# Steps for the compression rows and the query blocks in the mixing stage of a hybrid decoder block

## The chip, the cores and the metric

The kernel runs on one core of one Trainium2 chip. The metric is the device time of one execution in microseconds, as the median of several runs.

## The reference

The reference is one decoder layer on 512 positions of width 1024, in float32. It adds half a SwiGLU, then a mixing stage, then another half SwiGLU, then a gated embedding:

```python
h = h + 0.5 * swiglu(rmsnorm(h, norm_ffn1), ...)
z = rmsnorm(h, norm_mix) @ w_in        # q | k, v of three branches | gates | u
o = concat(nsa_attention(...), s5_mixer(u, ...))
h = h + o @ w_out
h = h + 0.5 * swiglu(rmsnorm(h, norm_ffn2), ...)
h = h + sigmoid(rmsnorm(h) @ w_ple_gate) * (p @ w_ple)
```

The attention has 8 heads of 64 in 2 groups, and three branches: compressed keys and values, selected blocks, and a window. At 512 positions with 8 blocks of 64 the selection takes all of them. The compressed branch takes windows of 32 positions, 16 apart (31 windows), adds a position table to each, and passes each window of 32 × 64 numbers through a small network with a gelu:

```python
blk = kv[:, tok] + pe                 # tok: 31 windows of 32 positions
compressed = gelu(blk @ w1) @ w2
```

The S5 mixer is a linear recurrence over time in 32 groups, then a gelu, and its output is gated: `y * sigmoid(y @ w_glu + b_glu)`.

## The kernel before

All products run on PE by one helper (`mm`, L133). Where full precision is needed, a float32 matrix is split in a part `hi`, that PE's fast form takes exactly, and a rest `lo`: ACT makes `hi` (L164), DVE makes `lo` (L166), and a product is three products. Raw weights (tile `raw`) come on ACT's DMA queue (L107). Most other transfers of the mixing stage go on SP's queue, in the order of its instructions.

The stages follow each other: the first SwiGLU to about 355 us, the mixing stage to about 604, the first half of the out product and the embedding to about 640, the second SwiGLU to about 995, the gate and the last norm to the end. The change lies in the mixing stage. That stage is a set of Python generators, each of which issues some instructions between two `yield`s:

- `s5_input` and `s5_all` (u, s): the S5 input and recurrence, in eight chunks (`s5_in`, L972 to L992, with the DVE operations L982 to L988 of tiles `t` and `vv`; `s5_out`, L998 to L1010; `s5_back`, L1016 to L1021, which makes the four tiles `yt`).
- `rotary` (L1044) and `keys` (k, L1059): projections, turned, sent to `qd` and `kd` in HBM, and for keys loaded back in four blocks `kf` of two transfers each. ACT makes `KA` (L1066), DVE `KB` (L1067).
- `cmp_kv` (z, L1072): the compression's keys and values, stored to `kcd` (L1082) and `vcd` (L1087).
- `v_gates` (v, L1091): values and gates, four blocks of 24 products each. DVE's L1106 and L1108 empty the sum's bank.
- `cmp_all` (c, L1130): the compression. `windows` (L1114) loads a source twice for each of the two groups, the second time shifted by a position, into tile `cst` (tags r1 and r2), and adds the position table on DVE (L1125) into tiles `cs` (keys) and `turn` (values). Then follow 32 products with `raw` in eight steps, a gelu, a transposition, the tile `chid` (npool's tag "acc", one buffer), and the products of `w2` and `chid` that make `KAc`, its copy `KBc` and `VLc`.
- `glu` (g, L1175): the gelu of the four `yt` tiles, in four steps with scratch `gt` (L916 to L924: Square on ACT, L922 on DVE, Tanh on ACT, L924 on DVE), then four sums of four products `yt`, `raw` in float32. The scratch takes the tags r1 and r2 in turn, the same as `cst`.
- `out_half` (f, L1195): the out product on the S5 half, eight blocks of 12 products.
- `queries` (p, L1219), once for each of the four blocks of 128 queries: loads the 4 heads of each half from `qd` twice, into partitions 0 to 63 and 64 to 127 of a tile `qf` (tag "ra", two buffers, shared with `kf`, the tiles of L1076 and L1086 and others). ACT scales into `QA` and `QB`, DVE makes the rest into the upper half of `QA` (L1240).
- `scores` (t, L1244): for each block and head the scores, a maximum on DVE (L1261) and exponentials on ACT (L916), of which only the sums are kept. `compressed` (x, L1267) does the same with `KAc`.
- `values` (V, L1326): the second pass with the sums known. PE makes scores into `ps_C` or `ps_B`, ACT exponentials `e` and `eh`, DVE `el` (L1359), PE the products with `VL` or `VLc` into `ps_D`.

The order in which the generators' steps are written is the table `PLAN` (L1590): each word is one step of one generator, with the block's number behind p, t, x, V. This order fixes which tile takes which buffer. A list scheduler then puts each engine's instructions into the order in which they will stand in the program, so that neither order is the same as `PLAN`.

Of the kernel before, what the change touches and what calls it, by code (L numbers as in the profile page):

```python
# [19 lines left out]
SEQ = 512  # L20
# [56 lines left out]
def block_kernel(ctx: ExitStack, tc: tile.TileContext, a: dict, out: bass.AP):  # L77
    nc = tc.nc
    V, S, G, PE = nc.vector, nc.scalar, nc.gpsimd, nc.tensor
# [15 lines left out]
    h = pers.tile([128, KT, SEQ], F32, name="h")  # L95
# [751 lines left out]
    def mixer(ctx):  # L847
# [7 lines left out]
        ind = mp.tile([128, 128], FR, name="ind")  # L855
# [61 lines left out]

        def gelu2(o, x, w, tag):

            t = tp.tile([128, SEQ], F32, tag=tag, name="gt")[:, :w]  # L920
            act(t, x, AF.Square)
            V.scalar_tensor_tensor(t, t, 1 / 0.044715, x, OP.add, OP.mult)  # L922
            act(t, t, AF.Tanh, scale=math.sqrt(2 / math.pi) * 0.044715)
            V.scalar_tensor_tensor(o, t, 1.0, x, OP.add, OP.mult)  # L924
# [189 lines left out]
        def windows(src, i, dst):  # L1114
            ev = []
            for g in range(2):
                st = tp.tile([128, SEQ], F32, tag=f"r{g + 1}", name="cst")
                nc.sync.dma_start(st[0:64], src[g])
                nc.sync.dma_start(st[64:128, 0:SEQ - 1], src[g, :, 1:SEQ])
                ev.append(st.rearrange("p (j l r) -> p l j r", l=8, r=2)[:, :, :, 0])  # L1120
            sp = []
            for half, t in enumerate(dst):
                t = t.rearrange("p (l g j) -> p l g j", l=8, g=2)
                for g in range(2):
                    V.tensor_tensor(t[:, :, g], ev[g],  # L1125
                                    pe[:, i, 8 * half:8 * half + 8, None].to_broadcast([128, 8, 32]), OP.add)
                sp.append(t)
            return sp

        def cmp_all():  # L1130

            kt = [tp.tile([128, SEQ], F32, tag=n, name="cs") for n in ("rb1", "r3")]
            sps = windows(kcd.rearrange("(g r) a t -> g (r a) t", g=2), 0, kt), windows(vcd, 1, (cosr, sinr))
            yield
            ps = bank("A", (128, 256))
            for l in range(16):
# [23 lines left out]
            kah = KAc[:, 0:128].rearrange("p (g i j) -> p g i j", g=2, i=2)  # L1160
            S.copy(kah[0:64, :, 0, 0:31], p)
            S.copy(kah[64:128, :, 0, 0:31], p)
            V.tensor_tensor(kah[0:64, :, 1, 0:31], p, kah[0:64, :, 0, 0:31].bitcast(F32), OP.subtract)
            for g in range(2):
                V.tensor_copy(KBc[0:64, :, g, 0:31],
                              kah[0:64, g:g + 1, 1, 0:31].bitcast(F32).to_broadcast([64, 4, 31]))
            for g in range(2):
                p = bank("D", (31, 64))
                for m in range(2):
# [46 lines left out]
        nmax = mp.tile([128, 4, 3, 8], F32, name="nmax")  # L1216
        den = mp.tile([128, 4, 3, 8], F32, name="den")

        def queries(qb, pool):  # L1219

            tq = slice(qb * 128, (qb + 1) * 128)
            QA = pool.tile([128, 8, 128], FR, tag="QA", name="QA", bufs=2)
            QB = pool.tile([128, 8, 128], FR, tag="QB", name="QB", bufs=2)
            envs[qb].update(QA=QA, QB=QB)
            if qb > 1:
                S.copy(QB[64:128], ind[64:128, None, :].bitcast(F32).to_broadcast([64, 8, 128]))
            else:

                G.dma_start(QB[64:128], ind[64:128, None, :].to_broadcast([64, 8, 128]))
            for i, (hs, st) in enumerate(zip((slice(0, 4), slice(4, 8)), STAGE[qb])):  # L1230
                src = qd[i].rearrange("(h r) a t -> (r a) h t", h=4)[:, :, tq]
                if st == "ra":
                    qf = mp.tile([128, 4, 128], F32, tag=st, name="qf", bufs=2)
                else:
                    qf = tp.tile([128, 4, 128], F32, tag=st, name="qf")
                nc.sync.dma_start(qf[0:64], src)
                nc.sync.dma_start(qf[64:128], src)
                S.activation(QA[:, hs], qf, AF.Copy, scale=0.125)
                S.activation(QB[0:64, hs], qf[0:64], AF.Copy, scale=0.125)
                V.scalar_tensor_tensor(QA[64:128, hs], qf[64:128], 0.125, QA[64:128, hs].bitcast(F32),  # L1240
                                       OP.mult, OP.subtract)
                yield

# [82 lines left out]
        def values(qb, env):  # L1326
# [3 lines left out]
            for g in range(2):  # L1330
# [39 lines left out]
                for par in range(2):  # L1370
# [7 lines left out]
        envs = {qb: {} for qb in range(4)}  # L1378
        gens = dict(u=s5_input(), k=keys(), q=rotary("q0", qd[0], TQ[0]), Q=rotary("q1", qd[1], TQ[1]), z=cmp_kv(),
                    v=v_gates(), s=s5_all(), c=cmp_all(), g=glu(), f=out_half(range(4, 8)))  # L1380
        made = {"p": lambda b: queries(b, mp if b > 1 else ap_), "t": lambda b: scores(b, TS[b]),
                "x": lambda b: compressed(b), "V": lambda b: values(b, envs[b])}
        table.append(tc.keep_in_program_order(S.preload_act_table_set("exp_and_others")))
        for step in PLAN.split():
# [195 lines left out]
TU, TQ, TW, TY, TP = "AD", "AA", "C", "D", "D"  # L1580

TS = "AB", "AB", "BC", "BBBBBBBBBCBCBCBC"
GT = "r1", "r2"
STAGE = ("ra", "ra"), ("ra", "ra"), ("ra", "ra"), ("ra", "ra")

PLAN = """u u u k s s u k k q s q s Q p3 s s s k s Q s t3 t3 s t3 z t3 s s t3 s p3 s z t3 t3 s s t3 t3 s g t3 g t3 g t3
v t3 c v v c t3 v c c p2 t2 t3 t3 t2 p2 c c c t2 c c t2 t2 c v t2 t2 t2 t2 t2 t2 t2 t2 t2 g close p1 p1 p0 x3  # L1590
# [169 lines left out]
```

## Time and profile before

| | us |
|---|---|
| median of 3 runs | 1046.03 |
| runs | 1049.57, 1046.03, 1044.05 |
| the profiled execution | 1045.87 |
| its span in the profile | 1044.1 |
| PE busy | 1030.6 |
| DVE busy | 823.1 |
| ACT busy | 502.0 |
| POOL busy | 160.5 |

The profile is of one execution. Its rows give a start, a duration, the engine (PE, PEld for the weight load that runs beside PE, DVE, ACT, POOL, SP; SPq is the time in which SP issues a DMA), the line of the kernel and the tiles, out<-in. A bracket holds the idle time ahead of it and what ended it. PE's durations overlap, since products are pipelined.

The mean granted clock of PE is 0.997 of full speed.

### The profile page before, as it was taken

The numbers are of one execution on the slowest core, as the hardware profiler recorded it, in microseconds if no ns is written. First come the engines' busy times: TensorE is split into PE (matmuls) and PEld (weight loads), VectorE is DVE, ScalarE is ACT, GpSimd is POOL, SyncE is SP. The second block draws the span as 40 slices with busy tenths as digits, with TensorE's granted clock in tenths as the row PEclk, the third lists the DMA queues.
The fourth block names the chain that finished last, engine by engine and source line by source line (L and its number), as shares of the span: only waits on it lengthen the run. The fifth ranks groups of instructions, "written<-read, shape, count | busy, mean of one in ns | idle before, by whom it ended". The sixth has DMA issues, their size and how long they took to land.

```text
span 1044.1 us, 15711 instructions
## 1 busy us (share of the span) xinstructions
PE 1030.6 (99%) x6049; PEld 876.9 (84%) x6049; DVE 823.1 (79%) x1381; ACT 502.0 (48%) x868; POOL 160.5 (15%) x181
## 2 busy tenths in 40 slices
PE   9999999999999999999999999999999999999997
PEld 7888888889889888776586688898899899899886
DVE  6798468988989766896689887996598588587666
ACT  6322232535336542477768855653365246245452
POOL 0003948207870200100000000000000000000001
PEclk9999999999999999999999999999999999999999
DMA  7424325636354648766610023434234333333412
GB/s 265 144 91 128 99 89 171 226 121 129 119 138 146 227 122 226 209 194 171 200 41 21 20 61 121 132 111 121 85 100 121 101 102 101 101 102 101 133 69 81
DMA packets 53114, 131.55 MB, mean 126 GB/s; under 512 B 10800, under 2 KB 19664, under 8 KB 53040
## 3 DMA queue, kind: packets, MB, share of 16 engines
q10 hardware_dynamic: 26352, 90.77, 27.4%
q0 software_dynamic: 6592, 18.48, 7.0%
q1 hardware_dynamic: 20096, 21.31, 6.7%
q8 instruction: 47, 0.77, 0.3%
q14 instruction: 27, 0.22, 0.1%
HBM read 114.39 MB, written 15.73 MB: 125 GB/s over the span
## 4 chain that ended last, share of the span: by engine, by line
PE 85%; DVE 5%; POOL 3%; DMA 3%; ACT 2%; issue 2%; SPq 0%; DVEq 0%; ACTq 0%; POOLq 0%
PE ps_A L133 25%; PE ps_C L133 24%; PE ps_B L133 20%; PE ps_D L133 15%; POOL ft L721 1%; POOL bt L720 1%; DMA qf<-qd 1%; DMA qd<-r 1%; DVE lo L166 1%; DMA kf<-kd 1%; DVE el L1359 0%; DMA cst<-kcd 0%; POOL ft L719 0%; DVE s L342 0%; POOL seen L559 0%
## 5 line engine op out<-in xcount | busy, mean ns | idle before, releaser
L164 ACT CAST hi<-raw 128x1024 fp32r<-128x1024 f32 (+2 forms) x143 | 144.4, 1010 | 253.3 <-PE ps_C L133 92.5
L133 PE MATMUL ps_C<-hq,hi 128*128 128x512 f32 x704 | 217.5, 390 | 0.2
L166 DVE TENSOR_TENSOR lo<-raw,hi 128x1024 fp32r<-128x1024 f32 (+2 forms) x143 | 173.4, 1213 | 42.5 <-ACT hi L164 41.5
L133 PEld LDWEIGHTS ps_C<-hq,hi 128*128 128x128 f32 x704 | 130.8, 188 | 28.1 <-DVE h L526 1.4
L133 PE MATMUL ps_C<-hq,lo 128*128 128x512 f32 x352 | 136.9, 389 | 0.0
L133 PE MATMUL ps_A<-xh,hi 128*128 128x512 f32 (+1 forms) x352 | 124.8, 355 | 0.4 <-ACT hi L164 0.4
L133 PE MATMUL ps_A<-xl,hi 128*128 128x512 f32 (+1 forms) x352 | 123.9, 352 | 0.0
L133 PE MATMUL ps_A<-xh,lo 128*128 128x512 f32 (+1 forms) x352 | 122.9, 352 | 0.2 <-DVE lo L166 0.2
L164 ACT CAST hi<-s 128x1024 fp32r<-128x1024 f32 x56 | 58.9, 1053 | 107.0 <-PE ps_D L133 60.9
L166 DVE TENSOR_TENSOR lo<-s,hi 128x1024 fp32r<-128x1024 f32 x56 | 70.6, 1261 | 20.3 <-ACT hi L164 20.2
L133 PEld LDWEIGHTS ps_C<-hq,lo 128*128 128x128 f32 x352 | 66.1, 188 | 13.8
L133 PEld LDWEIGHTS ps_A<-xh,hi 128*128 128x128 f32 x352 | 66.6, 189 | 10.3 <-ACT hi L164 0.7
L133 PEld LDWEIGHTS ps_A<-xh,lo 128*128 128x128 f32 x352 | 66.6, 189 | 9.2 <-DVE lo L166 0.4
L133 PEld LDWEIGHTS ps_A<-xl,hi 128*128 128x128 f32 x352 | 66.6, 189 | 9.3 <-DVE xl L192 0.3
L526 DVE SCALAR_TENSOR_TENSOR h<-ps_C,h 128x512 f32<-128x512 f32 x64 | 43.9, 686 | 36.5 <-PE ps_C L133 36.3
L133 PE MATMUL ps_B<-sh,lo 128*128 128x256 f32 x224 | 63.1, 282 | 0.3 <-DVE lo L166 0.3
L133 PE MATMUL ps_D<-sl,hi 128*128 128x256 f32 x224 | 63.1, 282 | 0.0
L133 PE MATMUL ps_B<-sh,hi 128*128 128x256 f32 x224 | 63.0, 281 | 0.0
L133 PE MATMUL ps_B<-sl,hi 128*128 128x256 f32 x224 | 62.9, 281 | 0.0
L133 PE MATMUL ps_B<-xh,hi 128*128 128x512 f32 (+1 forms) x168 | 62.9, 374 | 0.0
L133 PE MATMUL ps_D<-sh,hi 128*128 128x256 f32 x224 | 62.8, 280 | 0.0
L133 PE MATMUL ps_D<-sh,lo 128*128 128x256 f32 x224 | 62.6, 280 | 0.0
(434 smaller groups left out, 2472.1 us busy)
## 6 DMA issues: line engine op xcount, KB each, us to landing
raw<-in_wpack ACTq DMA_DIRECT2D x168, 512.0 KB, 3.6
si<-s5i POOLq DMA_DIRECT2D x8, 512.0 KB, 5.3
so<-s5o POOLq DMA_DIRECT2D x8, 512.0 KB, 5.7
h<-in_xT SPq DMA_DIRECT2D x8, 256.0 KB, 4.5
s5i<-fs POOLq DMA_DIRECT2D x1, 2048.0 KB, 11.4
xraw<-in_xT SPq DMA_DIRECT2D x8, 256.0 KB, 3.6
s5o<-gt POOLq DMA_DIRECT2D x1, 2048.0 KB, 13.3
s5i<-tcs POOLq DMA_DIRECT2D x2, 1024.0 KB, 10.2
```

The source lines that it names most:

```text
L133: return PE.matmul(o, lhsT, rhs, start=start, stop=stop, **kw)
L164: p, q = S.copy(hi[:, c], raw[:, c]), None
L166: q = V.tensor_tensor(lo[:, c], raw[:, c], hi[:, c].bitcast(F32), OP.subtract)
L526: V.scalar_tensor_tensor(h[:, m, :], o[m], 0.5, h[:, m, :], OP.mult, OP.add)
L720: G.tensor_tensor(bt, b2[:, 1], bc(psn[:, e]), OP.mult)
L721: G.tensor_tensor(ft[:, :, s_, :], ft[:, :, s_, :], bt, OP.add)
```

## The change

`windows` becomes a generator in two steps: the loads of both groups, and then the additions. `cmp_all` begins the keys' windows in one step, adds them and begins the values' windows in the next, and adds these in a third. In `PLAN` the first two of these steps stand earlier.

`queries` takes one tile for both halves of a block. Each half is loaded once, heads 0 to 3 into the lower 64 partitions, heads 4 to 7 into the upper. ACT and DVE then work on 64 partitions each, and the rows of `QA` for heads 4 to 7 have their main part above and the rest below. The loads are a step of their own, ahead of the work; for the last block (p3) the first half is loaded in its first step and the second in its second. `PLAN` has one more step of p2, p1 and p0 each, placed earlier. The table `STAGE` goes.

`glu`'s scratch `gt` moves from r1 and r2 to npool's tag "acc", of which there is one buffer, shared in turn with `chid`. `r1` and `r2` thereby have one user less. The low parts of `KAc` are written per group into the rows of that group, so that they match the new `QA`.

```diff
         def gelu2(o, x, w, tag):
-            t = tp.tile([128, SEQ], F32, tag=tag, name="gt")[:, :w]
+            t = (npool if tag == "acc" else tp).tile([128, SEQ], F32, tag=tag, name="gt", bufs=1)[:, :w]
...
         def windows(src, i, dst):
...
                 nc.sync.dma_start(st[64:128, 0:SEQ - 1], src[g, :, 1:SEQ])
                 ev.append(st.rearrange("p (j l r) -> p l j r", l=8, r=2)[:, :, :, 0])
+            yield
             sp = []
...
-            return sp
+            yield sp
...
         def cmp_all():
             kt = [tp.tile([128, SEQ], F32, tag=n, name="cs") for n in ("rb1", "r3")]
-            sps = windows(kcd.rearrange("(g r) a t -> g (r a) t", g=2), 0, kt), windows(vcd, 1, (cosr, sinr))
+            kw, vw = windows(kcd.rearrange("(g r) a t -> g (r a) t", g=2), 0, kt), windows(vcd, 1, (cosr, sinr))
+            next(kw)
+            yield
+            sps = [next(kw)]
+            next(vw)
+            yield
+            sps.append(next(vw))
             yield
...
-            V.tensor_tensor(kah[0:64, :, 1, 0:31], p, kah[0:64, :, 0, 0:31].bitcast(F32), OP.subtract)
             for g in range(2):
-                V.tensor_copy(KBc[0:64, :, g, 0:31],
-                              kah[0:64, g:g + 1, 1, 0:31].bitcast(F32).to_broadcast([64, 4, 31]))
+                low = kah[64 * g:64 * g + 64, g, 1, 0:31]
+                V.tensor_tensor(low, p[:, g], kah[0:64, g, 0, 0:31].bitcast(F32), OP.subtract)
+                V.tensor_copy(KBc[0:64, :, g, 0:31], low[:, None, :].bitcast(F32).to_broadcast([64, 4, 31]))
...
-        def queries(qb, pool):
+        def queries(qb):
...
-            for i, (hs, st) in enumerate(zip((slice(0, 4), slice(4, 8)), STAGE[qb])):
-                src = qd[i].rearrange("(h r) a t -> (r a) h t", h=4)[:, :, tq]
-                if st == "ra":
-                    qf = mp.tile([128, 4, 128], F32, tag=st, name="qf", bufs=2)
...
-                nc.sync.dma_start(qf[0:64], src)
-                nc.sync.dma_start(qf[64:128], src)
-                S.activation(QA[:, hs], qf, AF.Copy, scale=0.125)
-                S.activation(QB[0:64, hs], qf[0:64], AF.Copy, scale=0.125)
-                V.scalar_tensor_tensor(QA[64:128, hs], qf[64:128], 0.125, QA[64:128, hs].bitcast(F32),
+            if qb == 3:
+                QA, QB = make()
+            qf = mp.tile([128, 4, 128], F32, tag="ra", name="qf", bufs=2)
+            halves = slice(0, 64), slice(64, 128)
+            def load(i):
+                nc.sync.dma_start(qf[halves[i]], qd[i].rearrange("(h r) a t -> (r a) h t", h=4)[:, :, tq])
+            load(0)
+            if qb < 3:
+                load(1)
+                yield
+                QA, QB = make()
+            for i, r in enumerate(halves):
+                if i and qb == 3:
+                    load(1)
+                hs = slice(4 * i, 4 * i + 4)
+                S.activation(QA[r, hs], qf[r], AF.Copy, scale=0.125)
+                S.activation(QB[0:64, hs], qf[r], AF.Copy, scale=0.125)
+                V.scalar_tensor_tensor(QA[halves[1 - i], hs], qf[r], 0.125, QA[r, hs].bitcast(F32),
                                        OP.mult, OP.subtract)
                 yield
...
-GT = "r1", "r2"
-STAGE = ("ra", "ra"), ("ra", "ra"), ("ra", "ra"), ("ra", "ra")
+GT = "acc", "acc"
...
-PLAN = """u u u k s s u k k q s q s Q p3 s s s k s Q s t3 t3 s t3 z t3 s s t3 s p3 s z t3 t3 s s t3 t3 s g t3 g t3 g t3
+PLAN = """u u u k s s u k k q s q s Q p3 s s s k s Q s t3 t3 s t3 z t3 s s t3 s p3 s z c t3 t3 s s t3 t3 s g t3 c g t3 g t3
...
```

Four places show what this does to the programs of the engines. The first is DVE, where `cmp_kv`'s second projection is taken from its bank (L1086), between an operation of the S5 recurrence (L984) and its scan (L988). Before:

```order
L984 TENSOR_TENSOR t_4453<-ps_C,si 64x256
L1086 TENSOR_TENSOR ra<-ps_A,rb 128x512
L985 TENSOR_TENSOR t_4452<-t_4452,t_4453 128x256
L1261 TENSOR_REDUCE nmax<-ps_B 128x1
L166 TENSOR_TENSOR lo<-raw,hi 128x560
L1125 TENSOR_TENSOR cs<-cst,pe 128x8x32 x2
L988 SCALAR_TENSOR_TENSOR vv<-r_121,t_4452 128x64 x4
```

The same place after (the additions are L1126 there, the maximum L1279):

```order
L984 TENSOR_TENSOR t_4450<-ps_C,si 64x256
L1126 TENSOR_TENSOR cs<-cst,pe 128x8x32 x2
L985 TENSOR_TENSOR t_4449<-t_4449,t_4450 128x256
L1126 TENSOR_TENSOR cs<-cst,pe 128x8x32
L1086 TENSOR_TENSOR ra<-ps_A,rb 128x512
L1126 TENSOR_TENSOR cs<-cst,pe 128x8x32
L988 SCALAR_TENSOR_TENSOR vv<-r_121,t_4449 128x64 x4
L1279 TENSOR_REDUCE nmax<-ps_B 128x1
L166 TENSOR_TENSOR lo<-raw,hi 128x560
```

All four additions of the keys' windows stand together now (before, the second pair stood 16 rows further on), ahead of the last unit of the values' weights (`lo`, 128x560).

The second place is SP, around the store of the compression's keys (`kcd`). Before:

```order
L1082 DMA kcd<-ra 64x512 x2
L1118 DMA cst<-kcd 64x512
L1119 DMA cst<-kcd 64x511
L1236 DMA qf<-qd 64x4x128
L1237 DMA qf<-qd 64x4x128
L1087 DMA vcd<-ra 128x512
L1118 DMA cst<-vcd 64x512
L1119 DMA cst<-vcd 64x511
L1236 DMA qf<-qd 64x4x128
L1237 DMA qf<-qd 64x4x128
L1236 DMA qf<-qd 64x4x128
```

After:

```order
L1082 DMA kcd<-ra 64x512 x2
L1118 DMA cst<-kcd 64x512
L1119 DMA cst<-kcd 64x511
L1118 DMA cst<-kcd 64x512
L1119 DMA cst<-kcd 64x511
L1245 DMA qf<-qd 64x4x128 x2
L1087 DMA vcd<-ra 128x512
L1118 DMA cst<-vcd 64x512
L1119 DMA cst<-vcd 64x511
L1118 DMA cst<-vcd 64x512
L1119 DMA cst<-vcd 64x511
```

The second group's windows, which stood behind four pairs of `qf` loads, follow the first group's directly.

The third place is PE at the sums of `glu`, with the tiles' numbers: `yt_4135`, `yt_4276`, `yt_4434` and `yt_4569` are the four tiles of the gelu after the change, the last one `yts[3]`; `ps_A_5004` and `ps_A_5020` are the first two sums. Before, the third sum and what follows it were these, with `yt_4564` as `yts[3]`:

```order
L133 MATMUL ps_A_5049<-yt_4136,raw_5047 128x512
L133 MATMUL ps_A_5049<-yt_4277,raw_5047 128x512
L133 MATMUL ps_A_5049<-yt_4435,raw_5047 128x512
L133 MATMUL ps_A_5049<-yt_4564,raw_5047 128x512
L133 MATMUL ps_D_4882<-chid_4880,w2_3621 64x63 x2
L133 MATMUL ps_D_4890<-w2_3621,chid_4880 31x64 x2
```

After, from the last product of `chid`:

```order
L133 MATMUL ps_D_4893<-w2_3621,chid_4877 31x64 x2
L133 MATMUL ps_C_4939<-KA_3600,QA_4782 128x384
L133 MATMUL ps_C_4939<-KB_3601,QB_4783 128x384
L133 LDWEIGHTS identb_94
L133 MATMUL ps_C_4939<-maskq_3608,identb_94 128x128
L133 MATMUL ps_C_4951<-KA_3600,QA_4782 128x384
L133 MATMUL ps_C_4951<-KB_3601,QB_4783 128x384
L133 LDWEIGHTS identb_94
L133 MATMUL ps_C_4951<-maskq_3608,identb_94 128x128
L133 MATMUL ps_B_4981<-KAc_3604,QA_4101 128x64 x8
L133 LDWEIGHTS identb_94
L133 MATMUL ps_B_4981<-cmq_3610,identb_94 128x8x32
```

and, two more groups of scores further, from the product of 512 columns:

```order
L133 MATMUL ps_C_5319<-QA_4101,KAc_3604 128x512
L133 MATMUL ps_A_5004<-yt_4569,raw_5002 128x512
L133 MATMUL ps_A_5020<-yt_4569,raw_5002 128x512
L133 MATMUL ps_B_5067<-KA_3600,QA_4966 128x256
L133 MATMUL ps_B_5067<-KB_3601,QB_4967 128x256
```

In before a sum's four products stand together, and three sums are over ahead of the products of `chid`. After, the first three products of both sums stand ahead of those of `chid`, and their fourth, with `yts[3]`, comes after four groups of scores, eight compressed products and one product of 512 columns that follow the last product of `chid`.

The fourth place is PE at the first steps of the values, where `ps_D` takes the products with `VLc`. Before:

```order
L133 MATMUL ps_A<-oh,lo 128x512
L133 MATMUL ps_D<-eh,VLc 128x512
L133 MATMUL ps_C<-QA,KA 128x512
L133 MATMUL ps_C<-QB,KB 128x512
L133 MATMUL ps_C<-QA,KA 128x512
L133 MATMUL ps_C<-QB,KB 128x512
L133 MATMUL ps_D<-el,VLc 128x512
```

After:

```order
L133 MATMUL ps_D<-eh,VLc 128x512
L133 MATMUL ps_C<-QA,KA 128x512
L133 MATMUL ps_C<-QB,KB 128x512
L133 MATMUL ps_D<-el,VLc 128x512
L133 MATMUL ps_D<-eh,VL 128x512
L133 MATMUL ps_C<-QA,KA 128x512
L133 MATMUL ps_C<-QB,KB 128x512
L133 MATMUL ps_A<-oh,hi 128x512
L133 MATMUL ps_A<-ol,hi 128x512
L133 MATMUL ps_A<-oh,lo 128x512
```

The last blocks of the half out product (`oh`, `ol`) that stood ahead of the first values now stand between them.

More of the change, by code (lines that the diff above doesn't have):

```diff
@@ L1217, in mixer @@
         den = mp.tile([128, 4, 3, 8], F32, name="den")
-        def queries(qb, pool):
+        def queries(qb):
             tq = slice(qb * 128, (qb + 1) * 128)
[L1222 to L1229, printed above, removed]
-            for i, (hs, st) in enumerate(zip((slice(0, 4), slice(4, 8)), STAGE[qb])):
-                src = qd[i].rearrange("(h r) a t -> (r a) h t", h=4)[:, :, tq]
-                if st == "ra":
-                    qf = mp.tile([128, 4, 128], F32, tag=st, name="qf", bufs=2)
-                else:
-                    qf = tp.tile([128, 4, 128], F32, tag=st, name="qf")
-                nc.sync.dma_start(qf[0:64], src)
-                nc.sync.dma_start(qf[64:128], src)
-                S.activation(QA[:, hs], qf, AF.Copy, scale=0.125)
-                S.activation(QB[0:64, hs], qf[0:64], AF.Copy, scale=0.125)
-                V.scalar_tensor_tensor(QA[64:128, hs], qf[64:128], 0.125, QA[64:128, hs].bitcast(F32),
@@ new lines, in make @@
+            def make():
+                pool = mp if qb > 1 else ap_
+                QA, QB = (pool.tile([128, 8, 128], FR, tag=n, name=n, bufs=2) for n in ("QA", "QB"))
+                if qb > 1:
+                    S.copy(QB[64:128], ind[64:128, None, :].bitcast(F32).to_broadcast([64, 8, 128]))
+                else:
+                    G.dma_start(QB[64:128], ind[64:128, None, :].to_broadcast([64, 8, 128]))
+                envs[qb].update(QA=QA, QB=QB)
+                return QA, QB
+            if qb == 3:
+                QA, QB = make()
@@ L1380, in mixer @@
                     v=v_gates(), s=s5_all(), c=cmp_all(), g=glu(), f=out_half(range(4, 8)))
-        made = {"p": lambda b: queries(b, mp if b > 1 else ap_), "t": lambda b: scores(b, TS[b]),
+        made = {"p": queries, "t": lambda b: scores(b, TS[b]),
                 "x": lambda b: compressed(b), "V": lambda b: values(b, envs[b])}
@@ L1582 @@
 TS = "AB", "AB", "BC", "BBBBBBBBBCBCBCBC"
-GT = "r1", "r2"
-STAGE = ("ra", "ra"), ("ra", "ra"), ("ra", "ra"), ("ra", "ra")
-PLAN = """u u u k s s u k k q s q s Q p3 s s s k s Q s t3 t3 s t3 z t3 s s t3 s p3 s z t3 t3 s s t3 t3 s g t3 g t3 g t3
-v t3 c v v c t3 v c c p2 t2 t3 t3 t2 p2 c c c t2 c c t2 t2 c v t2 t2 t2 t2 t2 t2 t2 t2 t2 g close p1 p1 p0 x3
+GT = "acc", "acc"
+PLAN = """u u u k s s u k k q s q s Q p3 s s s k s Q s t3 t3 s t3 z t3 s s t3 s p3 s z c t3 t3 s s t3 t3 s g t3 c g t3 g t3
+v p2 t3 c v v c t3 v c c p2 t2 t3 t3 t2 p2 c c c p1 t2 c c t2 t2 c v t2 p0 t2 t2 t2 t2 t2 t2 t2 t2 g close p1 p1 p0 x3
 p0 g t2 g t2 g g t1 t1 x2 f S2 t1 f t1 t1 f t1 t1 f f t0 t0 R2 f x1 t0 R3 V3 V3 V3 V3 V3 V3 V3 V3 V3 V3 V3 V3
```

## The prediction

> **What bounds the kernel now.** First the page: its span and the busy time of each engine. Then the table of stretches over the mixing stage, whose columns are the stretch, its length, the busy time and count of PE, PEld, DVE, ACT and POOL, the granted clock, the DMA share and GB/s. Then the waits of PE, and a chain row for its pace.
>
> ```profile
> span 1044.1 us, 15711 instructions
> PE 1030.6 (99%) x6049; PEld 876.9 (84%) x6049; DVE 823.1 (79%) x1381; ACT 502.0 (48%) x868; POOL 160.5 (15%) x181
> 430.00:452.00 22.00, 20.48 (x146) 15.62 (x142) 18.11 (x39) 12.95 (x26) 2.96 (x5) 0.92 0.72 227
> 452.00:480.00 28.00, 28.00 (x212) 21.81 (x211) 23.37 (x46) 21.71 (x49) 2.57 (x4) 1.00 0.71 179
> 480.00:498.40 18.40, 17.18 (x122) 11.42 (x121) 11.96 (x24) 9.92 (x26) 0.00 (x0) 1.00 0.63 203
> 520.40:547.90 27.50, 27.50 (x164) 23.64 (x163) 23.77 (x56) 18.34 (x62) 0.00 (x0) 1.00 0.12 39
> 547.90:604.00 56.10, 55.47 (x221) 36.23 (x221) 50.36 (x105) 49.74 (x109) 0.00 (x0) 1.00 0.06 19
> 447.20:450.70 3.50, 3.50 (x25) 2.76 (x25) 2.90 (x6) 2.49 (x5) 0.00 (x0) 0.51 0.23 78
> 386.73 5.44 PE ps_A L133 x24
> PE ps_B L133 <- ACT ps_B L916: 1.4, 1, 1.4
> PE ps_A L133 <- PE ps_A L133: 0.7, 1, 0.7
> PE ps_A L133 <- DVE turn L1125: 0.5, 1, 0.5
> ```
>
> PE is the bound nearly throughout. The change touches about 430 to 604 us. There PE stands still in three places that the waits name: 1.4 + 0.7 + 0.5 = 2.6 us. A second, hidden loss is in the values stage (547.9 to 604). The chain's 24 products of 512 columns took 5.44 us, 0.227 us each. The stage's 221 instructions at that pace would need 50.2 us and took 56.1: 5.9 us lie in small waits that the busy share hides, as pipelined records overlap. A third is one window at half clock (0.51 over 3.5 us), worth 3.5 × 0.49 = 1.7 us. All that the change can win in its own stretch is therefore 2.6 + 1.7 + 5.9, about 10 us.
>
> The profiled execution took 1045.87 us, its span 1044.1 and 1.77 around it. That is 0.16 below the median of the runs shown, 1046.03, so the sum starts at 1045.87 and nothing is added at the end.
>
> **a. Loads of queries and keys, 420 to 447 us: 0.** In p3 each half now goes once into 64 partitions, and the one tile stays alive over both steps. It keeps one of the two "ra" buffers, so the third and fourth block of keys share the other.
>
> ```profile
> 432.82 0.44 SPq L1064 DMA_DIRECT2D kf<-kd  x1
> 434.04 0.66 DVE L1067 TENSOR_TENSOR KB<-kf,KA 64x512 fp32r<-64x512 f32 x1
> 439.46 0.68 DVE L1067 TENSOR_TENSOR KB<-kf,KA 64x512 fp32r<-64x512 f32 x1 [0.71 <-ACT KA L1066]
> 445.96 0.50 PE L133 MATMUL ps_B<-KA,QA 128*128 128x512 f32 x1 [1.37 <-ACT ps_B L916]
> qf<-qd SPq DMA_DIRECT2D x16, 128.0 KB, 3.3
> 518.95 0.20 DVE L1172 TENSOR_TENSOR VLc<-ps_D,VLc 31x64 fp32r<-31x64 f32 x1
> ```
>
> The fourth block's load started at 432.82; now it must wait for the KB of the third, which ends at 434.04 + 0.66 = 434.7. Its own KB and what DVE has queued behind it (the chain's next: rotary, the lo parts, two maxima) go 1.9 us later. The order puts a gelu pair ahead of it, which fills part of that, and PE's work in this stretch is mostly projections that need only weights. The delay then runs into the wait of part b, which absorbs it. PE's 1.37 us at 445.96 is a bank of scores not yet emptied and stays. I take 0; bounds 0 and +1.9. The eight DMAs fewer (qf from 16, the row above, to 8) and the low parts of KAc in two short instructions for one cost nothing on PE: SP and DVE have room at their places, covered by scores on PE. If that cover went, the second subtraction of KAc would add about 0.2 us (the last row, as small a tile) before a product that comes microseconds later.
>
> **b. Windows of the keys begun early: +1.6.** The loads move from after the queries' loads to straight behind the store of kcd, and the additions on DVE move ahead of the row of gates and values.
>
> ```profile
> 460.34 0.59 SPq L1119 DMA_DIRECT2D cst<-kcd  x1
> cst<-kcd SPq DMA_DIRECT2D x2, 128.0 KB, 4.1
> 462.47 0.43 DVE L984 TENSOR_TENSOR t<-ps_C,si 64x256 f32<-64x256 f32 x1
> 462.93 0.69 DVE L1086 TENSOR_TENSOR ra<-ps_A,rb 128x512 f32<-128x512 f32 x1
> 463.54 0.41 DVE L985 TENSOR_TENSOR t<-t,t 128x256 f32<-128x256 f32 x1
> 463.87 0.68 DVE L1261 TENSOR_REDUCE nmax<-ps_B 128x1 f32<-128x512 f32 x1
> 464.47 0.73 DVE L166 TENSOR_TENSOR lo<-raw,hi 128x560 fp32r<-128x560 f32 x1
> 465.12 1.09 DVE L1125 TENSOR_TENSOR cs<-cst,pe 128x256 f32<-128x256 f32 x2
> 466.14 0.82 DVE L988 TENSOR_TENSOR_SCAN vv<-r,t 128x64 f32<-128x64 f32 x4
> 469.20 0.29 PE L133 MATMUL ps_A<-lo,xh 128*128 128x280 f32 x1
> ```
>
> The same instructions stand on DVE up to L984 (462.47), only in another order, so DVE gets to the first addition at about 462.9. The first window can't be sent before the store of kcd is done, as in before: issued at 460.34, 4.1 us to landing, 464.4. DVE stands for about 1.5 to 2 us (2 if it is there at 462.5). Behind that wait are queued, in the new order, two additions (1.09), L985 (0.41), an addition (0.55), L1086 (0.69), an addition (0.55), L988 (0.82), a maximum (0.68) and the lo part of the last unit of v's weights (0.73): 464.4 + 5.5 = 469.9 instead of 465.2. PE's first product with that lo part is the 20th of the first v block. In before it came at 469.20; in the new order one group of scores (0.5) and one pair of s5 products (0.37) stand no longer ahead of it, so PE is there at 468.3. It waits 469.9 − 468.3 = 1.6 us. Low end 0, if the window lands when L984 ends; the high end is the whole 3.3 us that DVE once waited on such a load (the row at 480.31 below).
>
> [...]
>
> **c. The wait before compression goes: −1.2.**
>
> ```profile
> 480.31 1.11 DVE L1125 TENSOR_TENSOR cs<-cst,pe 128x256 f32<-128x256 f32 x2 [3.31 <-DMA cst<-kcd]
> 482.32 0.23 DVE L1108 TENSOR_SCALAR gp<-ps_A,ri 128x24 f32<-128x24 f32 x1
> 482.65 0.62 PE L133 MATMUL ps_A<-raw,cs 128*64 128x256 f32 x2 [0.69 <-PE ps_A L133]
> 485.27 0.43 PE L133 MATMUL ps_A<-raw,turn 128*64 128x256 f32 x1 [0.53 <-DVE turn L1125]
> ```
>
> DVE stood 3.31 us for the second key window, as its buffer came free late (it was gelu's scratch before). Behind it sat L1108, which frees the bank in which compression sums: PE started 0.33 us after it at 482.65 and had waited 0.69, though the profile names its own last product there. At 485.27 it waited 0.53 for the values' windows. Both additions now stand many rows earlier. −1.2; bounds −1.2 and 0 (another bank late instead).
>
> **d. The half clock: 0.** The one half-speed window behind the 1.37 us wait costs 1.7. Waits move about here, so it may go, stay or have a second: bounds −1.7 and +1.7, and I take the middle. [...]
>
> **e. One scratch for gelu: +0.5.** The fourth gelu of glu (yts[3]) now has the same buffer as chid and starts only after chid's last reader, the second w,chid product.
>
> ```profile
> L916 ACT ACTIVATE gt<-yt x4: 614/623/629, 447.9 to 482.7; 128x512 f32<-128x512 f32 x4
> L922 DVE SCALAR_TENSOR_TENSOR gt<-gt,yt x4: 683/692/694, 448.6 to 485.6; 128x512 f32<-128x512 f32 x4
> L924 DVE SCALAR_TENSOR_TENSOR yt<-gt,yt x4: 691/692/693, 450.0 to 489.1; 128x512 f32<-128x512 f32 x4
> 517.98 0.63 PE L133 MATMUL ps_B<-KAc,QA 128*128 128x64 f32 x4
> 518.45 0.42 PE L133 MATMUL ps_C<-KA,QA 128*128 128x384 f32 x1
> 518.93 0.42 PE L133 MATMUL ps_C<-KA,QA 128*128 128x384 f32 x1
> ```
>
> The chain is 0.62 + 0.69 + 0.62 + 0.69 = 2.6 us, and two maxima (each 0.68) stand inside it on DVE. In before it was over at 489.8, long before its use. PE's cover between that product and the first use of yts[3] is four groups of scores (518.45 to 518.93: 0.48 each), eight compressed products (2 × 0.47, from 517.98 to 518.45) and one of 512 columns (0.23): 3.1 us. If the maxima come in the shadow of the two ACT steps, the chain and its handovers need about 3.6 us, 0.5 too long. Bounds 0 and 2.6.
>
> **f. Out products between the first values: −1.5.** The four last blocks of the half-projection, 12 products each, and scores of the blocks 1 and 0 now stand among the first values instead of before them.
>
> ```profile
> PEld ps_D L133 <- DVE el L1359: 2.3, 11, 0.3
> PEld ps_D L133 <- ACT eh L916: 2.1, 5, 0.6
> ```
>
> These are the small waits of the values stage: PE runs out as DVE and ACT bring el and eh late. 48 × 0.227 = 10.9 us of other PE work now lies among them. But DVE has 23.77 + 50.36 = 74.1 us of work in the 83.6 us from 520.4 to 604, 89%, and PE can't be faster than DVE brings el. If that share went to 91% the two stretches would shorten by 2.1 us. I take −1.5; bounds −5.9 (all lost time filled) and 0.
>
> **The sum.** 0 + 1.6 − 1.2 + 0 + 0.5 − 1.5 = −0.6: 1045.87 − 0.6 = **1045.3 us**. The other stages keep their order and stay.
>
> **The rivals.**
>
> *Faster.* The values stage fills all its gaps (−5.9) and the half-clock window goes (−1.7), while b and c (+0.4 together) and e (+0.5) stay as above: 1045.87 − 5.9 − 1.7 + 0.9 = 1039.2. For it: 4.4 us of the lost 5.9 are waits of short length that one product each would hide. Against it: DVE would have to run at 74.1 / 77.7 = 95%.
>
> *Slower.* One mechanism: the single gelu buffer. If the last L924 comes later than 3.1 us after the second w,chid product, PE stands. The four groups of scores that are its cover each hand DVE a maximum (0.68) and ACT an exponential (about 0.62, as L916's row). If all of these go ahead of the chain's own steps, it takes 2.6 + 4 × 0.68 + 4 × 0.62 = 7.8 us; PE then stands 7.8 − 3.1 = 4.7, and behind so long a wait the clock goes to half for a window, 1.7. With no gain in f: 1045.87 + 0.4 + 4.7 + 1.7 = 1052.7. For it: chid's readers, DVE and ACT are all busy there. Against it: the order places the use of yts[3] behind four groups of scores, and two of the glu sums have their other three products done before.
>
> *Nothing happens.* Loads already start as early as a free buffer lets them, so the steps only move what PE doesn't see: c is given back as b, f gives nothing: 1045.9.
>
> **How the numbers follow.** The forecast case has 0.60, the faster rival 0.20, the slower 0.13, nothing 0.07. The bounds of the likeliest case (e 0 to 2.6, f −5.9 to 0, b 0 to 3.3, d ±1.7) added as independent give about ±4 around 1045.3. The range is 1038.5 to 1053.0: it takes in the forecast, the faster rival's nearer half and the slower rival up to its centre, and leaves out about 2 in 10. A measurement of this kernel can tell about 0.5%, 5.2 us (its three runs lie 5.5 us apart): faster means below 1040.8, slower above 1051.3. Below lies most of the faster rival (0.16) and an edge of the forecast (0.03): 0.19. Above lies the slower rival (0.11) and an edge (0.02): 0.13. The same has 0.68.
>
> **What would show it.** b: in the profile after, a DVE wait of 1.5 to 2 us for cst at the first addition, and PE waiting about 1.6 us at the 20th v product. c: no wait of PE at the first products of compression. e: a short PE wait before the first yts[3] product, named by L924. f: the values stretch with fewer PEld waits on el and eh; DVE above 90% there. It is wrong if PE stands several us before yts[3], if the values stage loses its 5.9 us whole, or if a and b leave a gap in the projections. If the stretches up to 420 us or behind 640 move, the cause lies outside what is costed here.

## The result and the profile after

The kernel after took 1052.16 us (median of 11 runs, 1049.48 to 1054.27), the kernel before 1046.03 (11 runs, 1044.05 to 1049.57). The ratio is 1.0056, with an interval of 1.0044 to 1.0068: about 6 us slower. The forecast of 1045.3 was wrong, though the time lies in its range. The profiled execution took 1053.12 us. Times are compared between executions at an undisturbed clock; one of the run with the gelu's scratch alone, 1266.77 us at a granted clock of 0.75, is left out.

First the lines of the page of the kernel after that answer to those of before:

```profile
span 1051.3 us, 15672 instructions
PE 1033.9 (98%) x6048; PEld 880.4 (84%) x6049; DVE 824.1 (78%) x1382; ACT 503.1 (48%) x868; POOL 159.6 (15%) x181
```

The span grew by 7.2 us. The work did not: there are 15672 instructions in place of 15711, and no engine is busy for more than 3.3 us longer. Now PE's waits in the kernel after (in all, times, longest), and then its table of stretches (stretch, length, the busy time and count of PE, PEld, DVE, ACT and POOL, granted clock, DMA share, GB/s), with one row of before ahead of it:

```profile
PE ps_B L133 <- ACT ps_B L916: 3.1, 2, 2.3
PE ps_A L133 <- DVE lo L166: 2.2, 2, 2.1
PE ps_A L133 <- DVE h L1217: 0.8, 2, 0.6
```

Before:

```profile
498.00:521.00 23.00, 23.00 (x101) 12.62 (x98) 16.12 (x31) 16.81 (x44) 0.57 (x1) 1.00 0.61 199
```

After:

```profile
468.90:475.70 6.80, 6.80 (x33) 4.98 (x31) 5.77 (x11) 4.88 (x13) 0.00 (x0) 0.50 0.91 227
498.00:521.00 23.00, 20.40 (x82) 12.47 (x80) 14.17 (x30) 14.50 (x40) 0.57 (x1) 0.78 0.44 149
509.90:520.10 10.20, 9.21 (x31) 6.33 (x32) 7.82 (x20) 7.06 (x23) 0.00 (x0) 0.50 0.14 56
547.81:614.95 67.14, 66.34 (x281) 47.17 (x279) 57.01 (x115) 56.10 (x129) 0.00 (x0) 1.00 0.09 25
```

Two waits of about 2 us are new (2.3 and 2.1 in the first two rows), and behind each PE runs at half clock (0.50): 6.8 us from 468.9 and 10.2 us from 509.9. Before had one such stretch of about 3.4 us (0.51 over 3.5 us in the prediction's row). Half of 6.8 + 10.2 is 8.5 us of PE time, against 1.7 before. In these two executions the clock thus takes up to 6.8 us more.

**The first wait** is the one forecast in part b. DVE and PE there, in the kernel after (start, duration, a bracket with the idle time ahead and what ended it):

```profile
459.95 0.43 DVE L984 TENSOR_TENSOR t<-ps_C,si 64x256 f32<-64x256 f32 x1
462.72 1.09 DVE L1126 TENSOR_TENSOR cs<-cst,pe 128x256 f32<-128x256 f32 x2 [2.34 <-DMA cst<-kcd]
467.23 0.73 DVE L166 TENSOR_TENSOR lo<-raw,hi 128x560 fp32r<-128x560 f32 x1
468.02 0.40 PE L133 MATMUL ps_A<-lo,xh 128*128 128x280 f32 x1 [2.06 <-DVE lo L166]
```

DVE stands 2.34 us at the first addition for its window. What is queued behind it, the lo part included, comes late, and PE waits 2.06 us at the product that was named. The size of this wait changes from execution to execution: in three of the runs below that have the same additions early it is 0.97, 1.04 and 0.77 us, and behind the 0.97 the clock is 1.00 (468.9 to 475.7).

**The second wait** was not forecast at its place. First three rows of PE before, where a sum of glu stands ahead of the products of `chid` and another behind three groups of scores:

```profile
507.67 3.65 PE L133 MATMUL ps_A<-yt,raw 128*128 128x512 f32 x8
511.25 0.44 PE L133 MATMUL ps_D<-chid,w 128*64 128x63 f32 x4
513.45 3.65 PE L133 MATMUL ps_A<-yt,raw 128*128 128x512 f32 x8
```

Now PE of the kernel after between the glu sums and the use of the last gelu, then ACT over the same time:

```profile
502.84 2.79 PE L133 MATMUL ps_A<-yt,raw 128*128 128x512 f32 x6
505.99 0.44 PE L133 MATMUL ps_D<-chid,w 128*64 128x63 f32 x4
508.07 0.22 PE L133 MATMUL ps_B<-maskq,identb 128*128 128x128 bf16 x1
510.58 0.69 PE L133 MATMUL ps_B<-KA,QA 128*128 128x384 f32 x1 [2.29 <-ACT ps_B L916]
516.35 0.67 PE L133 MATMUL ps_B<-KA,QA 128*128 128x384 f32 x1
517.23 0.67 PE L133 MATMUL ps_C<-KA,QA 128*128 128x384 f32 x1
518.72 2.67 PE L133 MATMUL ps_A<-yt,raw 128*128 128x512 f32 x4
523.00 7.03 PE L133 MATMUL ps_A<-yt,raw 128*128 128x512 f32 x16
```

```profile
508.37 1.04 ACT L164 CAST hi<-raw 128x1024 fp32r<-128x1024 f32 x1 [1.75 <-DMA raw<-in_wpack]
509.87 0.53 ACT L916 ACTIVATE ps_B<-ps_B,nmax 128x384 f32<-128x384 f32 x1
510.34 0.18 ACT L916 ACTIVATION_READ_ACCUMULATOR ps_B<-ps_B,nmax 128x1 f32 x1
512.43 0.62 ACT L916 ACTIVATE gt<-yt 128x512 f32<-128x512 f32 x1
515.18 0.61 ACT L916 ACTIVATE gt<-gt 128x512 f32<-128x512 f32 x1
```

PE waits for a bank of scores that ACT empties only at 510.34 + 0.18; ACT had stood 1.75 us at a cast whose weights had not landed. The next groups of scores run at half pace: from 516.35 to 517.23 one takes 0.88 us, where the prediction's rows have 0.48. The fourth gelu starts at 512.43, 6.3 us before PE takes it at 518.72, and the last eight products of glu (x16, as the records count two per product) stand in one block at 523.

### The profile page after: what moved, and what is told of

It reads as the page before. It is cut to its first block, busy times and chain, and to the rows that moved or that the text cites. A ratio compares the mean times of both kernels' runs of the same rounds, so it can differ in the third digit from the quotient of the medians.

```text
span 1051.3 us, 15672 instructions
## 1 busy us (share of the span) xinstructions
PE 1033.9 (98%) x6048; PEld 880.4 (84%) x6049; DVE 824.1 (78%) x1382; ACT 503.1 (48%) x868; POOL 159.6 (15%) x181
## 4 chain that ended last, share of the span: by engine, by line
PE 80%; DVE 6%; DMA 4%; POOL 3%; ACT 3%; issue 3%; SPq 0%; DVEq 0%; ACTq 0%; POOLq 0%
PE ps_A L133 24%; PE ps_C L133 23%; PE ps_B L133 19%; PE ps_D L133 14%; DMA raw<-in_wpack 2%; DVE lo L166 1%; POOL ft L721 1%; ACT hi L164 1%; POOL bt L720 1%; DMA kf<-kd 1%; DMA kd<-r 1%; DVE QB L1341 0%; DVE aa L349 0%; DVE s L342 0%; POOL ft L719 0%
```

## Theories

Theory A: the fourth gelu, queued behind `chid` in one buffer, makes the loss. Its late end moves the glu products that used to stand among the scores, and leaves a thin stretch, in which PE has little else to run while it waits for banks, with a wait and half clock. The early additions add a smaller wait of the same kind. Rival B: the new loads of queries or the windows make it, and the buffer is innocent. Rival C came up with the traces: the waits matter as such, or the half clock behind them does.

## The experiments

All were run beside the kernel before on the same chip. Ratios are to that kernel, with 95% intervals; its median was 1045.19 to 1046.17 in these comparisons. The kernel after was not run again beside them, so a difference to it sets two comparisons side by side; where the ratios give another amount than the medians, both are given.

**The fourth gelu apart.**

```diff
-GT = "acc", "acc"
+GT = "acc", "acc", "acc", "r1"
...
-                gelu2(yt, yt, SEQ, GT[m % 2])
+                gelu2(yt, yt, SEQ, GT[m])
```

> The kernel after, with the fourth gelu's scratch on tag r1 in place of the buffer shared with chid; the first three keep the shared one. Theory A (two long PE waits in the kernel after, each followed by several half-clock windows, make the 6 us; the one at 508 us comes because the late fourth gelu moved the sums of glu behind it, so that PE is early at a score whose bank ACT has not emptied): the wait of 2.29 us at 508 and its three half-clock windows go, the one at 466 us (2.06 us, two windows) stays: about 1048 us. Rival B (the loads of queries and keys in 64 partitions, or the windows, cost the time, and the gelu buffer is innocent): 1052 us as the kernel after.

Measured 1045.26 us, ratio 1.0001 (0.999 to 1.0011). The loss is gone with one tile's place (6.9 us by the medians, 5.8 by the ratios). This stretch in its profile:

```profile
498.00:521.00 23.00, 23.00 (x99) 12.68 (x99) 16.19 (x32) 16.66 (x43) 0.57 (x1) 1.00 0.60 183
```

PE is busy throughout at full clock. The time came out lower than expected. In the profiled execution the half clock near 469 us was gone too (1.00 from 468.9 to 475.7), with a wait of 0.97 us left there.

**The additions behind the lo part.** The step of the additions stands one place later in `PLAN`, and they wait for their turn:

```diff
+                    with tc.issue_after(state["vlo"][-1].ins) if i == 0 else nullcontext():
+                        V.tensor_tensor(t[:, :, g], ev[g],
+                                        pe[:, i, 8 * half:8 * half + 8, None].to_broadcast([128, 8, 32]), OP.add)
...
```

> The kernel after, with the additions of the keys' windows held behind the lo part of the last unit of the values' weights on DVE, and their step one place later in the table. Theory A: PE's wait of 2.06 us for that lo part at 466 us goes, with the two half-clock windows behind it (6.83 us at 0.50, 3.4 us lost at most): 1047 to 1049 us, with the wait at 508 us still there. Rival B (the half clock there is hidden behind DVE's own lateness, so that taking the wait away only moves it): 1051 to 1052 us.

Measured 1049.11 us, ratio 1.0036 (1.0021 to 1.005): 3 us better than the kernel after, 2 by the ratios. The first wait is gone, the second is as in the kernel after (2.6 us at most). PE now waits 2.07 us for `so` at 457.68, and no half clock follows that wait: products of 512 columns start 0.23 us apart behind it, at 459.04 and 459.27.

**Both edits.**

> Both edits of the first two runs together. Theory A: no PE wait over 1 us and at most one half-clock window in the mixing stage: 1043 to 1046 us, so at or below the kernel before, since what the change frees (the waits at compression, the out products between the values) is then kept. Rival B (something else of the change costs about 6 us, as the queries' loads): 1050 us or more.

Measured 1043.7 us, ratio 0.9982 (0.997 to 0.9993). Both kernels are beaten, the one before by about 2 us. PE in the two stretches:

```profile
460.00:500.00 40.00, 39.19 (x285) 27.83 (x283) 28.01 (x56) 28.64 (x66) 1.98 (x3) 1.00 0.69 204
498.00:521.00 23.00, 23.00 (x106) 13.74 (x105) 17.38 (x34) 17.16 (x45) 0.00 (x0) 1.00 0.48 146
```

**The cast later**, the gelu left late.

```diff
+                state["vlc"] = S.copy(VLc[0:31, g, 0:64], p).ins
...
+                        with (tc.issue_after(state["oh"]) if done and m == 4 else
+                              tc.issue_after(state["vlc"]) if not done and m == 4 else nullcontext()):
```

> The kernel after, with one pinned instruction: ACT's cast of the third weight unit of the half out product comes behind the copy of the last VLc. The late gelu stays late. Theory A, its second half (ACT stands 1.75 us in that cast for its load while the exponentials that free PE's bank are queued behind it): the wait at 508 us shrinks from 2.29 to under 1 us, its three half-clock windows become one or none: 1047 to 1050 us. Rival C (the late gelu itself starves PE there, whatever ACT's order): the wait moves to the next use of the gelu's last tile and the time stays at 1051 to 1053 us.

Measured 1050.52 us, ratio 1.0045 (1.0033 to 1.0057), 1.6 us under the kernel after, between the two expectations; the intervals of the two ratios overlap. In its profile, PE and then ACT:

```profile
510.17 0.69 PE L133 MATMUL ps_C<-KA,QA 128*128 128x384 f32 x1 [1.42 <-ACT ps_C L916]
```

```profile
507.99 0.62 ACT L916 ACTIVATE gt<-yt 128x512 f32<-128x512 f32 x1
508.52 1.03 ACT L164 CAST hi<-raw 128x1024 fp32r<-128x1024 f32 x1
509.45 0.53 ACT L916 ACTIVATE ps_C<-ps_C,nmax 128x384 f32<-128x384 f32 x1
```

The cast no longer stands waiting for its weights, but it and the late gelu's first step still run ahead of the exponential that empties the other bank, and PE waits for that one. ACT's order still has a part in the wait, so this run does not separate it from the thin stretch.

**The gelu's scratch alone on the shared buffer**, all four steps, in the kernel before.

```diff
...
-GT = "r1", "r2"
+GT = "acc", "acc"
```

> The kernel before with one part alone: the gelu's scratch on the one buffer shared with chid (all four steps); windows, queries and the table of steps as before. Its program already has the fourth product of two glu sums behind the products of chid. Theory A (this sharing is the cause): 1049 to 1052 us, with a PE wait of about 2 us near 508 us at a score's bank and two or three half-clock windows behind it. Rival B (the sharing costs only together with the new steps and loads): 1045 to 1047 us.

Measured 1054.28 us, ratio 1.0073 (1.0057 to 1.0088), above the expected range. The same kernel was run again for a trace:

> The same kernel as the run of the gelu's scratch alone, for a profile at full clock. Theory A: span about 1052 us, PE waits of 1 to 2.5 us between 500 and 515 us at a score's bank and at least two half-clock windows behind them; and, since r1 and r2 are free, the additions for the first windows stand ahead of the values' last lo part, so that a second wait of 1 us or more lies there.

1050.93 us, ratio 1.0047 (1.0026 to 1.0069). PE waits 1.53 us for ps_C at 510.52, with about 10 us at half clock behind it (the mean clock of this execution is 0.994). The additions do stand ahead of the lo part, and DVE waits 2.51 us there, but the second wait of PE that was expected is only 0.50 us at the most. This one part makes the loss without any other. Why the same kernel lay 3 us apart in the two runs stays open.

**`chid` apart**, the gelu's four steps on their one buffer.

```diff
-            hid = npool.tile([128, SEQ], F32, tag="acc", name="chid", bufs=1)[:, :256].rearrange("p (m c) -> p m c", m=2)
+            hid = tp.tile([128, SEQ], F32, tag="r2", name="chid")[:, :256].rearrange("p (m c) -> p m c", m=2)
```

> The kernel after, with chid in a tile of its own (tag r2) and the gelu's scratch still on one buffer for all four steps. If it is the order gelu behind chid that costs, this is as the run with the fourth gelu on r1: 1044 to 1046.5 us, no half-clock window near 510 us. If it is that one buffer serves four gelus in turn, it stays at 1050 us or more.

Measured 1045.25 us, ratio 0.9987 (0.9977 to 0.9998), and no half clock near 510 us in its profile, whose mean clock is 0.998. One buffer for four gelus costs nothing; standing behind `chid` does.

**The windows' part alone** in the kernel before, with both cures (the additions behind the lo part, the fourth gelu on r1).

> The kernel before with the windows' part alone (steps of their own, begun early), the additions held behind the lo part as in the run of that name, and the fourth gelu on r1; the queries' loads as before. If the windows bring the gain of the run with both edits (1043.7 us): 1043 to 1045 us, with no PE wait before compression. If the gain comes from the queries' loads: 1045 to 1046.5 us, as before.

Measured 1044.6 us, ratio 0.9982 (0.997 to 0.9994), the same ratio as with the queries' part beside it. The gain over before comes from the windows, with the gelu's first three scratches off r1 and r2, which this run has too.

**The queries' part alone** in the kernel before.

> The kernel before with the queries' part alone (each half loaded once, steps ahead, KAc's low parts in the rows of their group); gelu's scratch and windows as before. If the queries' part costs nothing, as the prediction had it (term a at 0, bounds 0 and +1.9): 1045 to 1047 us, with the waits before compression (0.7 and 0.5 us) as before. If it costs by the late loads of the second half in p3, where ACT stands with the copies of so behind it: 1047 us or more, with a PE wait of 1.5 to 2 us for so.

Measured 1052.54 us, ratio 1.0051 (1.0032 to 1.007). Slow, but not as expected: PE has no wait for `so`. In its profile:

```profile
448.66 0.63 ACT L916 ACTIVATE gt<-yt 128x512 f32<-128x512 f32 x1 [2.58 <-DMA qd<-r]
467.64 1.08 DVE L1125 TENSOR_TENSOR cs<-cst,pe 128x256 f32<-128x256 f32 x2 [3.30 <-DMA cst<-kcd]
471.29 0.50 PE L133 MATMUL ps_B<-KA,QA 128*128 128x512 f32 x1 [2.83 <-ACT ps_B L916]
```

The additions again stand early on DVE, ahead of a maximum, and PE waits for the bank. So they were pinned behind the lo part here too:

> The queries' part alone, with the additions of the keys' windows held behind the lo part of the last unit of the values' weights. If the 6.5 us of the queries' part alone were DVE's wait of 3.30 us for the first window (467 us) and what it held up, this is 1045 to 1048 us, and PE's wait of 2.83 us at 471 us is gone. If the queries' loads themselves cost, it stays at 1050 to 1053 us.

Measured 1049.66 us, ratio 1.0031 (1.002 to 1.0043). This lies between the two expectations: 2 to 3 of the 5.3 to 6.5 us go with that wait. In the trace that is left, gelu's scratch on r1 waits for the rotated queries to be sent from r1 (ACT stands 3.00 us there, 2.58 without the pin, 1.35 in the kernel before); PE then waits 1.33 us for `yt` and 1.68 us for a bank, and from 454.6 on runs 6.8 us at a granted clock of 0.51, worth up to 3.4 us. It also waits 1.8 us for the values' windows. These were not tested one by one.

**`chid` apart and the additions pinned.**

> The kernel after with chid in a tile of its own (r2) and the additions held behind the lo part; the gelu's scratch on its one buffer. Theory A: as the run with both edits, 1043 to 1045 us, under the kernel before. Otherwise 1045 us or more.

Measured 1043.94 us, ratio 0.998 (0.997 to 0.9991): the other way to the faster kernel.

**The fourth gelu alone on the shared buffer**, in the kernel before.

```diff
...
-GT = "r1", "r2"
+GT = "r1", "r2", "r1", "acc"
```

> The kernel before with one tile moved: the scratch of the fourth gelu alone lies on the buffer shared with chid, the first three stay on r1 and r2, so that the windows, the queries and all up to the middle of compression stand as before. Theory A: this alone makes most of the loss, 1049 to 1053 us, with the order of PE as in the kernel after (fourth product of two glu sums behind the products of chid) and half-clock windows near 510 us. Rival B: 1045 to 1047 us.

Measured 1050.13 us, ratio 1.0027 (1.001 to 1.0044), its nine runs spread from 1046.09 to 1051.49. Its profiled execution is the slowest of them, 1051.49 us. Up to the middle of compression the order is that of before. PE's waits between the first product of `chid` and 513 us, and a stretch behind them:

```profile
507.35 0.44 PE L133 MATMUL ps_D<-chid,w 128*64 128x63 f32 x4 [0.62 <-ACT chid L1154]
511.46 0.44 PE L133 MATMUL ps_C<-KA,QA 128*128 128x384 f32 x1 [0.25 <-ACT ps_C L916]
512.64 0.44 PE L133 MATMUL ps_B<-KA,QA 128*128 128x384 f32 x1 [0.49 <-ACT ps_B L916]
```

```profile
513.70:520.50 6.80, 6.80 (x23) 4.73 (x23) 3.86 (x10) 4.16 (x14) 0.00 (x0) 0.50 0.17 64
```

No wait is over 0.62 us, and still 6.8 us at half clock follow. The granted clocks of the nine go with their times: the three fastest (1046.09 to 1047.74) have 0.998 or 0.999, the others (1048.29 to 1051.49) 0.995 to 0.997. That left the question of what costs: the waits or the clock.

**Fillers.** Products of zero weights are added to the open first glu sum, which they leave as it is. They stand among the groups of scores between the products of `chid` and the late glu products. With seven of them ACT keeps its order there; with fourteen the late gelu's first step comes behind two more groups' exponentials than in the kernel after, so the fillers are then not the only change.

```diff
...
+                    if (m, k) == (0, 3):
+                        for j in range(7, len(state[2])):
+                            with tc.issue_after(state[2][j]):
+                                mm(o, zb, maskq[:, None, :].to_broadcast([128, 4, 128]), False, False)
                     mm(o, raw[:, q * 128:(q + 1) * 128], yts[k], k == 0, k == 3)
...
```

> The kernel after with seven products of zero weights (512 columns, 0.227 us each, 1.6 us in all) added to the open first glu sum among the groups of scores between the first and last products of chid, three of them where PE waited 2.29 us; all else in the order of the kernel after. They change nothing in the sum. If the half clock (10.24 us at 0.50) carries the loss: with fewer idle stretches one or two of the three half-clock windows go and the time falls by 1 to 4 us, to 1048 to 1051 us, though there is more work. If the loss is the waiting itself: the fillers lie in the waits and the time stays at 1051.5 to 1052.5 us; if ACT's and DVE's rate sets it, with no room, it rises to 1053.5 us.

Measured 1049.72 us, ratio 1.004 (1.0027 to 1.0052), 2.4 us under the kernel after, 1.7 by the ratios, whose intervals overlap. Its profiled execution has a mean clock of 0.946 against 0.995 to 0.996 in the other four, so its stretches are not set beside the others.

> The same with two such products at each place, fourteen in all, 3.2 us of PE work, six of them (1.4 us) where PE waited 2.29 us. If the half clock carries the loss: no half-clock window near 510 us, 1046 to 1050 us. If not: 1052 to 1055 us.

Measured 1048.07 us, ratio 1.0025 (1.0012 to 1.0038), 4.1 us under the kernel after, 3.2 by the ratios, with 3.2 us more of PE work. The place in its profile, and the same stretch as above:

```profile
505.74 1.67 PE L133 MATMUL ps_A<-maskq,zb 128*128 128x512 bf16 x7
508.02 0.44 PE L133 MATMUL ps_B<-KA,QA 128*128 128x384 f32 x1 [0.61 <-ACT ps_B L918]
```

```profile
509.90:520.10 10.20, 10.10 (x52) 6.49 (x52) 8.94 (x21) 9.25 (x28) 0.00 (x0) 1.00 0.26 94
```

The clock is 1.00 where it was 0.50, and 52 records lie in the stretch that held 31. The last gelu still comes behind `chid`. (At the first wait this execution, of a mean clock of 0.997, has 3.4 us of half clock and the kernel after, of 0.991, has 6.8, though the order there is the same; a part of the 4.1 us may be that.)

> The run with the fourth gelu alone on the shared buffer, with the fourteen zero products. If the half clock (6.83 us at 0.50 there, 3.4 us lost) carries the loss: under that run by 1 us or more, about 1047 to 1049 us. If not: 1050 to 1053 us.

Measured 1050.2 us, ratio 1.0047 (1.0034 to 1.0061): no gain over the run without fillers. By its own expectation that speaks against the half clock. Its profiled execution, the fastest of five (1048.06 us, mean clock 0.998), has no half clock in the mixing stage, where the one without fillers (1051.49 us, 0.995) had 6.8 us of it; but the median doesn't follow.

## Why the prediction was wrong

**e, the step that failed.** It was put at +0.5 with bounds 0 and 2.6. Taking the sharing out of the kernel after brought 6.9 us (1052.16 to 1045.26 and 1045.25; by the ratios 5.8 and 7.2); putting it alone into the kernel before cost 4.0 us with the fourth gelu (1050.13 against 1046.17; 2.8 by the ratio) and 4.8 to 8.2 with all four. The working counted only PE's cover ahead of the first use of yts[3]. Both of its terms came out longer, and they met: the chain took 6.2 us (512.43 to 518.66) in place of 3.6, and PE, at half clock, took 6.5 us over its cover (512.21 to 518.72) in place of 3.1. Its waits name none of note there. In the profile with seven fillers, at its clock of 0.95, PE waits 0.28 us at that product, by the last step of the gelu on DVE, so the 0.5 was of the right size for what it counted. What it left out is what the moved products had been covering. A group of scores takes PE 0.48 us; ACT's exponentials of such groups start 0.55 us apart at best (512.96 and 513.51 in the kernel after), and ACT also stands at casts whose weights have not landed, 2.26 and 1.75 us in this stretch of the kernel after. Before, it stood 1.22 and 1.50 us at such casts there, and PE had glu products to run meanwhile.

**d** was put at 0 with bounds of ±1.7, as if one more stretch of 3.5 us were all that could come. The trace has 17.0 us at half clock in place of 3.4, 6.8 us more of lost PE time at most. The other executions agree. Their granted clock is on record, and (1 − clock) × time is a bound for what the clock takes: in the mean 7.1 us for the eleven of the kernel after, 2.6 and 2.1 with the fourth gelu or `chid` apart, 2.3 to 3.2 for the kernel before. The mean time of the kernel after lies 5.8 us over that of the kernel before, so up to 4 or 5 of these go with the clock. The fillers show that this is not only a sign of the waiting: with fourteen of them the half clock near 510 us is gone, and the kernel is 3.2 to 4.1 us faster with more work, though ACT's order differs there too. So the clock likely carries more of the loss of the kernel after than the wait does. For the kernel with the fourth gelu alone the same count doesn't say so: 3.3 us against 2.6 for the kernel before beside it, of 3.1 us in mean time. The lengths of 6.8 and 10.2 us are two and three times the 3.4 seen before. What sets these lengths, no run shows.

**The slower rival** named the right buffer and came within 1 us (1052.7), at 0.13. That its number fits is in part luck, as its mechanism was half right: one gelu buffer behind `chid`, no gain kept, half clock behind a wait. Its wait of 4.7 us before yts[3] did not come; 2.3 us at a score's bank and 10.2 us at half clock came in its place.

**b** held: a DVE wait of 2.34 us (1.5 to 2 forecast), a PE wait of 2.06 us at the 20th product (1.6 forecast). Its price, from the run without the sharing to that with both cures, is 1.6 us (1045.26 to 1043.7). In the kernel after, where half clock follows it, taking it away brought 2 to 3 us. The transfer itself was shorter than the 4.1 us taken: from its issue at 459.95 to 462.72, 2.8 us. DVE stood as long because it was there at 460.4, and not at 462.9 as the prediction had it. The same load took 4.1 us in the kernel before and 4.7 us in the run with the queries' part alone (issued at 462.90, and DVE released by it at 467.64), so the one reading of 4.1 us did not settle it.

**c** held: in the kernel after no wait stands before compression, where 0.7 and 0.5 us were. With both cures the kernel is 2 us faster than before, the run with the windows alone as well.

**a** at 0 is right for the kernel after and wrong for the part alone. Beside the windows' part the queries' part neither gains nor costs (0.9982 with and without it). Alone, with gelu's scratch still on r1 and r2, it costs 6.5 us (5.3 by the ratio), 2 to 3 of them by early additions.

**f** was −1.5. By the same count as in the prediction the stretch of the values lost 56.24 − 220 × 0.227 = 6.3 us before (551.47 to 607.71) and 67.14 − 281 × 0.227 = 3.4 after:

```profile
551.47:607.71 56.24, 55.60 (x220) 36.12 (x219) 50.20 (x105) 48.67 (x104) 0.00 (x0) 1.00 0.06 18
```

```profile
551.69:607.95 56.26, 55.61 (x221) 36.10 (x219) 50.19 (x105) 48.69 (x105) 0.00 (x0) 1.00 0.05 18
```

The first row is before, the second the run with the fourth gelu apart. There the out products stand ahead of the values again, and the gain is gone. So it was no gain of the change, but work that the late gelu had pushed down.

What stays open: which of the waits in its trace makes the 3 us of the queries' part alone that the pin does not give back; what makes most of the loss in the kernel with the fourth gelu alone, whose mean clock left the fillers little to win; and how much of the second wait is ACT's order at the casts. PE's waits of 1.3 to 2.1 us for `so` near 457 us, in the profiles of seven of these runs and of neither kernel, are not explained either.

## What to carry to other kernels

When a buffer is shared, ask not only whether its last user is ready in time, but what independent work its lateness pulls out from between other instructions; that work may be what kept another engine's pace from showing. A stretch where PE waits a little at every group can cost more by the clock behind it than by the waits: the wait of 2.29 us here, with half of the 10.2 us behind it, took up to 7.4 us, about three times its length. It need not be so: another wait (2.07 us, the additions behind the lo part) had no half clock behind it. And when a load is begun earlier, its consumer should not simply move up to meet it: DVE stood 2.34 us at the early addition here, with the lo part queued behind it, and PE waited 2.06 us for that part; held behind the work that was there, the same early load came with a gain of 2 us.

## What was not expected of the hardware

Waits of 0.62 us at most, spread over a few us, were followed by 6.8 us at half clock (the fourth gelu alone), while a wait of 2.07 us in another run was followed by none. Fourteen products that compute nothing came with a kernel 3.2 to 4.1 us faster and a clock of 1.00 where it was 0.50.
